# Opening of a bidirectional encoder layer: the first RMSNorm sums its squares over partitions in two groups of four chunks, and VectorE squares one of the chunks

## The chip, the cores and the metric

The kernel runs on one core of one Trainium2 chip. The metric is the device time of one execution in microseconds (us), shown as the median of several runs; the profile is of one further execution. Engines are called as in the profile: PE is TensorE's matmuls, PEld TensorE's weight loads, DVE is VectorE, ACT is ScalarE, POOL is GpSimd, SP is SyncE, which here does nothing but issue DMAs.

## The reference

One layer with 512 tokens of width 1024, all float32. Three sublayers each begin with an RMSNorm whose output is scaled and shifted by vectors computed from a conditioning vector c:

```python
c_act = silu(c)
mod = c_act @ w_mod + b_mod
sh1, sc1, g1, sh2, sc2, g2, sh3, sc3, g3 = split(mod, 9)
h = rmsnorm(x, norm_ffn1) * (1 + sc1) + sh1      # the opening
x = x + 0.5 * g1 * swiglu(h, w_ffn1_in, w_ffn1_out)
# then two gated attention mixers on one normalised input, then a second SwiGLU like the first
# rmsnorm(x, g) = x * rsqrt(mean(x * x, axis=-1) + 1e-6) * g
```

The change touches only the sum of squares of the very first RMSNorm.

## The kernel before, in words

The residual stream lies with features on partitions: eight chunks `x[0]` to `x[7]`, each of 128 features by 512 tokens. A sum over the 1024 features of a token is therefore a sum over eight chunks and then over 128 partitions. The sum over partitions is done by PE: `Norm.sums` (L321) takes a chunk of squares, 128 tokens at a time, as the weights and a two-column tile of ones as the moving operand, so a call is four matmuls of two columns each into the bank `tp`. Every float32 matmul shows as two passes in the trace, so a call is eight weight loads and eight matmuls there.

The opening (L586 to L648) is written out by hand: under a manual schedule PE, DVE, ACT, SP and POOL take their instructions in the order of the code. The steps:

- SP issues the loads of the eight chunks (L224), then those of the columns of `w_mod` (L234) and of the first weights (L191); ACT's queue issues the loads of c and of the parameters.
- PE spreads c over all partitions by two matmuls with one row (L590), and then does twelve matmuls of the identity by itself, whose result nobody reads (`warm(12)`, L596). They stand in PE's queue ahead of the sums.
- ACT squares the eight chunks, one after the other as they land (L631). DVE adds each square to the running sum (L633), so that one chunk of sums is left. In between DVE does four small operations on parameters (L250, L255).
- ACT applies silu to the spread c (L636); the result `cact` goes to a scratch in memory by a DMA from POOL (L637), and DVE needs it for every column.
- PE sums the one chunk over partitions (L638, through L326), does six more `warm` matmuls, and waits.
- ACT scales the sums (L305), POOL raises them to the power -0.5 (L306), PE spreads the result `rs` over partitions through the identity (L315).
- DVE meanwhile computes columns of the conditioning (`mod_col`, L269): SC1 of chunk 0 and SH1 of chunk 0; then a tiny copy of `rs` (L643), which makes it wait for POOL; then SC1 of chunk 1; and then the first operation of the hidden activations (L335).
- ACT rounds that result (L336), and PE starts on the first products of the first SwiGLU (L654). The eight chunks of the hidden activations follow in the same manner (`first_chunk`, L661).

Buffers: `sq` takes a tile of the ring `f2` of eight tiles for each chunk.

Of the kernel before, what the change touches and what calls it, by code (L numbers as in the profile page):

```python
# [14 lines left out]
AF = mybir.ActivationFunctionType  # L15
ALU = mybir.AluOpType
# [108 lines left out]
def layer(ctx: ExitStack, tc: tile.TileContext, a: dict):  # L125
    nc = tc.nc
    V, S, G, PE = nc.vector, nc.scalar, nc.gpsimd, nc.tensor
# [11 lines left out]
    def xt():  # L139
        return sbuf("x", [P, T], F32, 8)  # L140

    def f2():
        return sbuf("f2", [P, T], F32, F2)
# [61 lines left out]
    FULL = (slice(0, T),)  # L205
# [15 lines left out]
    x = [xt() for _ in range(NC)]  # L221
# [38 lines left out]
    def mod_col(v, c, w=None):  # L260
        if w is None:
            w = mod_load(v, c)
        t, b = modv[v][:, c : c + 1], mod_begin(v)[:, c : c + 1]
        cact = at_c[0]
        if v in norms:
            by = par[:, norms[v] + c : norms[v] + c + 1]
        else:
            by = 1.0 if v in (SH1, SH2, SH3) else -0.5 if v == G1 or v == G3 and c % 4 < 2 else 0.5
        summed = V.tensor_tensor_reduce(  # L269
            out=w, in0=w, in1=cact, scale=by, scalar=b, op0=ALU.mult, op1=ALU.add, accum_out=t,  # L270
        )
        if len(at_c) > 1:
            tc.keep_in_program_order(summed)
# [354 lines left out]
    n1 = Norm()  # L628
    for c in range(NC):
        sq = f2()  # L630
        S.activation(sq, x[c], AF.Square)  # L631
        if c:
            V.tensor_tensor(sq, sq, before, ALU.add)  # L633
        before = sq
    for i in range(2):
        S.activation(cact[:, i * T : (i + 1) * T], cb[i], AF.Silu)  # L636
    G.dma_start(c_scr, cact[0:1, :])  # L637
    n1.sums(sq, FULL[0], True, True)  # L638
    mod_col(SC1, 0, w1[0][0])
    rs = n1.rstd(FULL[0], S)  # L640
    first_split(0)
# [978 lines left out]
    x = [xt() for _ in range(NC)]  # L1620
# [375 lines left out]
```

## Time and profile before

| what | value |
|---|---|
| median of 3 runs | 1053.09 us |
| lowest, highest | 1052.79, 1056.16 us |
| the profiled execution, its time | 1054.45 us |
| its span (first to last instruction) | 1052.7 us |
| PE busy | 1037.4 us, 99% of the span |
| DVE, ACT, POOL busy | 75%, 56%, 14% |
| DMA moved | 214.07 MB, mean 203 GB/s |

The profile holds a page with the busy time of each engine, and views that can be asked of the trace: instructions in order of time (start, duration, engine, line, operation, output<-inputs, count, and in brackets the idle time before and what ended it), a table of who waited for whom, and the chain of work that ended last, followed back from the end. Times are counted from the start of the span; the profiled execution's own time is 1.75 us longer than the span. Ends of matmuls are modelled, so for PE the starts are the better measure. An engine that is idle off the chain costs nothing.

### The profile page before, as it was taken

Reading aid. Unit: us, or ns where it says so; the run is one execution under the profiler, and the core shown is the slowest. Engines: PE = TensorE matmul, PEld = TensorE weight load, DVE = VectorE, ACT = ScalarE, POOL = GpSimd, SP = SyncE. Lnnn points to the kernel's source line nnn. Section 1 sums busy time; section 2 is a strip of 40 time slices with the busy share of each in tenths; the row PEclk is TensorE's granted clock in tenths of the full one; section 3 lists DMA queues with packets and bytes.
Section 4 is the critical chain, followed back from the end, with each engine's and each line's share of the span. In section 5 each row is a group of like instructions: output and inputs, shape, how many; then the busy total and the mean of one; then the engine's idle time right before and its main releaser. Section 6 shows DMA issues by size and latency. Waiting matters only on the chain.

```text
span 1052.7 us, 18398 instructions
## 1 busy us (share of the span) xinstructions
PE 1037.4 (99%) x7216; PEld 952.2 (90%) x7216; DVE 792.9 (75%) x1421; ACT 591.3 (56%) x976; POOL 151.7 (14%) x166
## 2 busy tenths in 40 slices
PE   8999999999999999999999999999999999999997
PEld 6799899989998988888888888989999999999997
DVE  7988767687967844677964778995888777877777
ACT  6565235424653443787755878435867545655553
POOL 1100001001001100441012401001111111111210
PEclk9999999999999999999999999999999999999999
DMA  9977886788666384785358875795578999999964
GB/s 353 364 211 231 255 247 145 203 290 199 176 200 210 131 268 142 159 195 114 89 172 203 217 181 149 280 323 132 111 177 197 236 250 198 206 236 210 210 137 125
DMA packets 64760, 214.07 MB, mean 203 GB/s; under 512 B 7713, under 2 KB 9889, under 8 KB 64674
## 3 DMA queue, kind: packets, MB, share of 16 engines
q1 hardware_dynamic: 43920, 143.63, 39.7%
q0 software_dynamic: 18304, 65.02, 33.9%
q10 hardware_dynamic: 2450, 4.25, 1.1%
q8 instruction: 56, 0.92, 0.4%
q14 instruction: 30, 0.25, 0.1%
HBM read 203.96 MB, written 8.92 MB: 202 GB/s over the span
## 4 chain that ended last, share of the span: by engine, by line
PE 88%; DVE 5%; ACT 3%; DMA 1%; issue 1%; POOL 1%; SPq 0%; DVEq 0%; ACTq 0%; POOLq 0%
PE acc L436 7%; PE acc L434 7%; PE acc L435 7%; PE sc L436 6%; PE sc L434 6%; PE sc L435 6%; PE sc L166 5%; PE sc L164 5%; PE sc L165 5%; PE acc L164 3%; PE acc L165 3%; PE acc L166 3%; PE acc L1148 2%; PE acc L1150 2%; PE acc L1149 2%; PE tp L1199 1%
## 5 line engine op out<-in xcount | busy, mean ns | idle before, releaser
L436 PE MATMUL acc<-b,low 128*128 128x256 f32 x614 | 170.1, 277 | 0.2 <-DVE low L170 0.2
L434 PE MATMUL acc<-b,high 128*128 128x256 f32 x614 | 170.0, 277 | 0.1
L435 PE MATMUL acc<-b,high 128*128 128x256 f32 x614 | 169.9, 277 | 0.2 <-DVE b L1776 0.2
L434 PE MATMUL sc<-b,high 128*128 128x256 f32 x542 | 149.9, 277 | 1.2 <-DVE f L516 1.2
L436 PE MATMUL sc<-b,low 128*128 128x256 f32 x542 | 150.0, 277 | 0.1
L435 PE MATMUL sc<-b,high 128*128 128x256 f32 x542 | 149.8, 276 | 0.0
L436 PEld LDWEIGHTS acc<-b,low 128*128 128x128 f32 x614 | 115.3, 188 | 0.7 <-DVE low L170 0.6
L435 PEld LDWEIGHTS acc<-b,high 128*128 128x128 f32 x614 | 115.3, 188 | 0.5 <-DVE b L1776 0.4
L434 PEld LDWEIGHTS acc<-b,high 128*128 128x128 f32 x614 | 115.4, 188 | 0.4 <-issue 0.3
L434 PEld LDWEIGHTS sc<-b,high 128*128 128x128 f32 x542 | 101.8, 188 | 1.4 <-issue 1.3
L436 PEld LDWEIGHTS sc<-b,low 128*128 128x128 f32 x542 | 101.7, 188 | 0.3 <-DVE low L801 0.3
L435 PEld LDWEIGHTS sc<-b,high 128*128 128x128 f32 x542 | 101.8, 188 | 0.0
L164 PE MATMUL sc<-b,high 128*128 128x512 f32 (+1 forms) x272 | 99.1, 364 | 0.0
L166 PE MATMUL sc<-b,low 128*128 128x512 f32 (+1 forms) x272 | 98.8, 363 | 0.2 <-DVE low L895 0.2
L165 PE MATMUL sc<-b,high 128*128 128x512 f32 (+1 forms) x272 | 98.9, 364 | 0.0
L482 DVE TENSOR_TENSOR low<-raw,high 128x1024 fp32r<-128x1024 f32 (+1 forms) x60 | 70.2, 1187 | 34.9 <-ACT high L481 34.8
L164 PE MATMUL acc<-b,high 128*128 128x512 f32 (+1 forms) x200 | 72.6, 363 | 0.2 <-DVE f L1597 0.2
L482 DVE TENSOR_TENSOR low<-u,high 128x1024 fp32r<-128x1024 f32 (+1 forms) x47 | 55.8, 1188 | 22.4 <-ACT high L481 22.2
L166 PE MATMUL acc<-b,low 128*128 128x512 f32 (+1 forms) x200 | 71.8, 359 | 0.0
L165 PE MATMUL acc<-b,high 128*128 128x512 f32 (+1 forms) x200 | 71.8, 359 | 0.0
L269 DVE CUSTOM_DVE_ANT_0 u<-u,ka,begin 128x1024 f32<-128x1024 f32 x45 | 58.6, 1310 | 12.4 <-DMA u<-w_mod 12.3
L481 ACT CAST high<-raw 128x1024 fp32r<-128x1024 f32 (+1 forms) x60 | 59.6, 1021 | 0.3 <-PE acc L435 0.3
(403 smaller groups left out, 2791.4 us busy)
## 6 DMA issues: line engine op xcount, KB each, us to landing
u<-w_mod SPq DMA_DIRECT2D x66, 512.0 KB, 6.0
raw<-w2i SPq DMA_DIRECT2D x31, 512.0 KB, 5.2
u<-w2i POOLq DMA_DIRECT2D x31, 512.0 KB, 7.4
raw<-w1u SPq DMA_DIRECT2D x27, 512.0 KB, 5.7
u<-w1u POOLq DMA_DIRECT2D x18, 512.0 KB, 7.7
raw<-w1o SPq DMA_DIRECT2D x16, 512.0 KB, 4.4
raw<-w_gate SPq DMA_DIRECT2D x16, 512.0 KB, 4.1
low<-w_gate POOLq DMA_DIRECT2D x13, 512.0 KB, 7.3
```

The costliest lines, as they stand in the source:

```text
L164: PE.matmul(out, wh, xh, start=first, stop=False)
L165: PE.matmul(out, wh, xl, start=False, stop=False)
L166: PE.matmul(out, wl, xh, start=False, stop=last)
L269: summed = V.tensor_tensor_reduce(out=w, in0=w, in1=cact, scale=by, scalar=b, op0=ALU.mult, op1=ALU.add, accum_out=t,)
L434: PE.matmul(out, wh[:, s], xh, start=first and j == 0, stop=False, skip_group_check=True)
L435: PE.matmul(out, wh[:, s], xl, start=False, stop=False, skip_group_check=True)
L436: PE.matmul(out, wl[:, s], xh, start=False, stop=last and j == 1, skip_group_check=True)
L481: S.copy(hi, t)
L482: V.tensor_tensor(lo, t, f(hi), ALU.subtract)
L1148: PE.matmul(out[t][:, 0:n], hh[k][:, ht], wh[:, o : o + n], start=k == 0, stop=False)
L1149: PE.matmul(out[t][:, 0:n], hh[k][:, ht], wl[:, o : o + n], start=False, stop=False)
L1150: PE.matmul(out[t][:, 0:n], hl[k][:, ht], wh[:, o : o + n], start=False, stop=k == NC - 1)
```

## The change

The fourth chunk (c is 3) is squared by DVE instead of ACT. The running sum of squares starts anew at the fifth chunk (c is 4), so that there are two partial sums: of chunks 0 to 3 and of chunks 4 to 7. Each is summed over partitions by itself: `n1.sums` is called once inside the loop, right after the fourth chunk, which opens the accumulation, and once at its old place, which closes it.

```diff
     for c in range(NC):
         sq = f2()
-        S.activation(sq, x[c], AF.Square)
-        if c:
+        if c == 3:
+            V.tensor_tensor(sq, x[c], x[c], ALU.mult)
+        else:
+            S.activation(sq, x[c], AF.Square)
+        if c % 4:
             V.tensor_tensor(sq, sq, before, ALU.add)
         before = sq
+        if c == 3:
+            n1.sums(sq, FULL[0], True, False)
     for i in range(2):
         S.activation(cact[:, i * T : (i + 1) * T], cb[i], AF.Silu)
     G.dma_start(c_scr, cact[0:1, :])
-    n1.sums(sq, FULL[0], True, True)
+    n1.sums(sq, FULL[0], False, True)
     mod_col(SC1, 0, w1[0][0])
```

Five lines are added, so lines behind the loop are numbered five higher in the changed kernel.

PE's order from the start of the program to the spread of `rs` (`sc` and `tp`, `op` are banks, `f_…` the chunk of squares, `sm` the tile of `rs`), before:

```order
L590 MATMUL sc_121<-u_2_76,ones 128x512
L590 MATMUL sc_122<-u_2_76,ones 128x512
L596 MATMUL sc_125<-ident 128x128 x12
L326 MATMUL tp_183<-ones,f_37_177 128x2 x4
L596 MATMUL sc_197<-ident 128x128 x6
L315 MATMUL op_204<-ident,sm_189 128x128 x4
```

And with the change:

```order
L590 MATMUL sc_121<-u_2_76,ones 128x512
L590 MATMUL sc_122<-u_2_76,ones 128x512
L596 MATMUL sc_125<-ident 128x128 x12
L326 MATMUL tp_168<-ones,f_33_165 128x2 x4
L326 MATMUL tp_168<-ones,f_38_181 128x2 x4
L596 MATMUL sc_200<-ident 128x128 x6
L315 MATMUL op_207<-ident,sm_192 128x128 x4
```

Four matmuls of two columns are added behind the twelve `warm` matmuls, and those of the old place stand behind them.

DVE's order from its first addition to the first column, before:

```order
L633 TENSOR_TENSOR f_31_159<-f_31_159,f_30_157 128x512
L250 SCALAR_TENSOR_TENSOR begin<-par 128x8
L255 TENSOR_SCALAR begin<-par 128x2x2
L633 TENSOR_TENSOR f_32_162<-f_32_162,f_31_159 128x512
L255 TENSOR_SCALAR begin<-par 128x2x2
L633 TENSOR_TENSOR f_33_165<-f_33_165,f_32_162 128x512
L633 TENSOR_TENSOR f_34_168<-f_34_168,f_33_165 128x512
L633 TENSOR_TENSOR f_35_171<-f_35_171,f_34_168 128x512
L633 TENSOR_TENSOR f_36_174<-f_36_174,f_35_171 128x512
L633 TENSOR_TENSOR f_37_177<-f_37_177,f_36_174 128x512
L269 ISA u_21_138,mod_97<-u_21_138,ka_112,begin,par 128x1024
```

And with the change:

```order
L636 TENSOR_TENSOR f_31_159<-f_31_159,f_30_157 128x512
L250 SCALAR_TENSOR_TENSOR begin<-par 128x8
L255 TENSOR_SCALAR begin<-par 128x2x2
L636 TENSOR_TENSOR f_32_162<-f_32_162,f_31_159 128x512
L632 TENSOR_TENSOR f_33_165<-x_81 128x512
L255 TENSOR_SCALAR begin<-par 128x2x2
L636 TENSOR_TENSOR f_33_165<-f_33_165,f_32_162 128x512
L636 TENSOR_TENSOR f_36_175<-f_36_175,f_35_173 128x512
L636 TENSOR_TENSOR f_37_178<-f_37_178,f_36_175 128x512
L636 TENSOR_TENSOR f_38_181<-f_38_181,f_37_178 128x512
L269 ISA u_21_138,mod_97<-u_21_138,ka_112,begin,par 128x1024
```

DVE still does seven operations on 128x512 tiles: the square of the fourth chunk (L632, reading `x_81`) has come, and the addition that joined the fifth chunk to the running sum has gone. On ACT one of the eight squares has gone; nothing else is moved.

## The prediction

> **What bounds the kernel now.** The page comes first: PE is busy nearly throughout.
>
> ```profile
> span 1052.7 us, 18398 instructions
> PE 1037.4 (99%) x7216; PEld 952.2 (90%) x7216; DVE 792.9 (75%) x1421; ACT 591.3 (56%) x976; POOL 151.7 (14%) x166
> ```
>
> Of the 15.3 us that PE is idle (1052.7 - 1037.4), the table of waits (waiter, releaser, total us, times, longest) puts these among the five longest:
>
> ```profile
> PE sc L590 <- DMA u<-c: 2.3, 1, 2.3
> PE acc L654 <- ACT b L336: 1.4, 2, 0.8
> ...
> PE op L315 <- POOL sm L306: 0.9, 1, 0.9
> ```
>
> All three lie in the opening. So the opening is a chain in front of a PE-bound kernel, and what it gains or loses passes to the end if nothing behind absorbs it. The chain of waits for the first 30 us (start, duration, what):
>
> ```profile
> 2.32 3.75 PE sc L590 x4
> 6.07 5.26 PE sc L596 x24
> 11.33 0.85 PE tp L326 x8
> 12.18 0.02 issue
> 12.20 0.27 ACT sm L305
> 12.48 0.08 issue
> 12.56 1.87 POOL sm L306
> ...
> 14.53 1.17 DVE u L269
> 15.70 0.09 issue
> 15.79 0.09 DVE mod L269
> 15.88 0.66 DVE b L335
> ...
> 29.42 0.67 DVE b L335
> ```
>
> The reader is to see what stands ahead of the sums (L326): not DVE's additions (L633), but the twelve `warm` matmuls (L596). Behind the sums come ACT, POOL, and then DVE up to 30 us, without a DMA. The last gap of the opening on PE, from the instructions in order of time:
>
> ```profile
> 30.89 0.50 PE L654 MATMUL acc<-b,high 128*128 128x512 f32 x1 [0.56 <-ACT b L336]
> ```
>
> From there the chain runs on PE's own products.
>
> Whether DVE or PE holds the sums back is the question on which this change hangs, since both are ready within a tenth of a microsecond. PE, its weight loads, and DVE in order of time:
>
> ```profile
> 6.00 5.33 PE L596 MATMUL sc<-ident 128*128 128x128 f32 x24
> 10.64 0.69 PE L596 MATMUL sc<-ident 128*128 128x128 f32 x3
> 11.17 1.00 PE L326 MATMUL tp<-ones,f 128*128 128x2 f32 x8
> 12.03 1.58 PE L596 MATMUL sc<-ident 128*128 128x128 f32 x12
> 11.11 0.97 PEld L326 LDWEIGHTS tp<-ones,f 128*128 128x128 f32 x8
> 12.00 0.53 PEld L596 LDWEIGHTS sc<-ident 128*128 128x128 f32 x4
> 7.18 3.88 DVE L633 TENSOR_TENSOR f<-f,f 128x512 f32<-128x512 f32 x5 [0.70 <-ACT f L631]
> 10.37 0.69 DVE L633 TENSOR_TENSOR f<-f,f 128x512 f32<-128x512 f32 x1
> 10.97 1.34 DVE L269 CUSTOM_DVE_ANT_0 u<-u,ka,begin 128x1024 f32<-128x1024 f32 x1
> ```
>
> DVE's last addition ends at 10.37 + 0.69 = 11.06. The `warm` passes run back to back from 6.00; the last three lie from 10.64 to 11.33 by the modelled ends, and the weight loads of the sums begin at 11.11 with no idle time in front. So before the change both releases came together, and the sums cannot start before about 11.1 even if DVE were done long before.
>
> **The change part by part.** *ACT loses one square.* Its row, the transfers that it waits for, and ACT's two silus behind:
>
> ```profile
> 6.52 3.32 ACT L631 ACTIVATE f<-x 128x512 f32<-128x512 f32 x5 [0.85 <-DMA x<-x]
> 9.21 0.63 ACT L631 ACTIVATE f<-x 128x512 f32<-128x512 f32 x1
> 9.75 1.07 ACT L636 ACTIVATE ka<-sc 128x512 f32<-128x512 f32 x2
> L224 SPq DMA_DIRECT2D x<-x x8: 382/430/432, 0.7 to 4.0; - x8
> DMA to landing us min/median/max: 2.8/4.4/5.2
> ```
>
> The last chunk is issued at 4.0 and the longest transfer takes 5.2 us, so it lands near 9.2, where ACT's last square starts (9.21). The five squares from 6.52 start (9.21 - 6.52) / 4 = 0.67 us apart, although one takes 0.63: they follow the landings. So taking one away leaves ACT's last square at 9.21 to 9.84 and its silus at 9.75 to 10.82. I take 0 for this part; its other bound would be 0.63 earlier, if the chunks lay there already.
>
> *DVE takes one square and drops one addition.* The square of chunk 3 needs only its landing, 6.52. An addition in a row costs (3.88 - 0.69) / 4 = 0.80 us from start to start. The square starts at 6.52, the addition of chunk 3 near 7.4 (0.80 and the small L255 between), that of chunk 5 when ACT has squared it (6.52 + 3 x 0.67 = 8.53), those of chunks 6 and 7 0.80 apart, 9.33 and 10.13. The last ends at 10.82, a quarter of a microsecond before 11.06. The first column (L269 at 10.97) needs ACT's silu, which ends at 10.82 as before, so it doesn't move.
>
> *PE gets four more matmuls of two columns.* They need the sum of chunks 0 to 3, ready near 8.1, but stand behind the `warm` matmuls and so start at 11.11. Eight passes take from 11.11 to 12.00 in the weight-load rows: 0.89 us. The old call then starts at 12.00 instead of 11.11; its data is there since 10.82. It ends 0.89 us later. Nothing hides this term: PE is the chain here. DVE's quarter microsecond is worth nothing, because PE isn't free to use it.
>
> *What is queued behind.* The rows of the engines that wait:
>
> ```profile
> 12.20 0.27 ACT L305 ACTIVATE sm<-tp,eps 128x4 f32<-128x4 f32 x1 [1.39 <-PE tp L326]
> 14.33 1.04 ACT L614 CAST high<-raw 128x1024 fp32r<-128x1024 f32 x1 [1.86 <-DMA raw<-w1s]
> 12.56 1.86 POOL L306 TENSOR_TENSOR sm<-sm,half 128x4 f32<-128x4 f32 x1 [0.78 <-ACT sm L305]
> 14.45 0.17 DVE L643 COPY sm<-sm 128x4 f32<-128x4 f32 x1 [0.93 <-POOL sm L306]
> 14.47 1.16 PE L315 MATMUL op<-ident,sm 128*128 128x128 f32 x8 [0.86 <-POOL sm L306]
> 17.35 0.50 PE L654 MATMUL acc<-b,high 128*128 128x512 f32 x1 [0.83 <-ACT b L336]
> ```
>
> ACT was idle for 1.39 before L305, and its next work, L614, waits for a DMA until 14.33: L305 at 13.09 to 13.36 still fits in front. POOL's power goes from 12.56 to 13.45, DVE's copy, for which DVE sat idle 0.93, from 14.45 to 15.34, the column and L335 behind it too, and PE's first product from 17.35 to 18.24. L614 ends at 15.37, long before ACT's next turn, so it absorbs nothing. From 14.5 to 30.9 the chain runs on DVE work and two waits on it; no step of it waits for a clock or a transfer that stays in place. So 0.89 arrives at 30.89 and passes to the end.
>
> *The sum.* 0 + 0 + 0.89, about +0.9 us. The profiled execution would have a span of 1053.6 and a time of 1054.45 + 0.9 = 1055.3; its time was 1.36 above the median, so for the median I forecast 1053.09 + 0.9 = 1054.0.
>
> *Bounds of the added matmuls.* The unknown is how fast PE runs when it reaches them. The 24 early passes go at about (10.64 - 6.00) / 22 = 0.21 us each, the twelve later ones at 1.58 / 12 = 0.13. If the early passes ran at 0.13 in another execution, they would end at 9.1, the first sums at 10.0, and the second would start with DVE, 10.82 against 11.1: -0.3 us. If the eight new passes ran at 0.21, they would cost 1.7. I take 0.89, measured at just this place, and keep -0.3 and +1.7 as ends. The granted clock doesn't explain the two rates:
>
> ```profile
> 6.00:11.00 5.00, 5.00 (x24) 5.00 (x24) 3.88 (x8) 4.12 (x7) 0.00 (x0) 1.00 0.98 379
> ```
>
> PEclk, third from the end, reads 1.00 over the slow stretch. [...] The pace of these rows agrees with a doubling near 11.0, which the granted clock alone would not tell. [...]
>
> **The rivals.** *PE speeds up earlier* than in this profile. For it: the rate changed just before the sums, so it can't be a fixed property of the place. Against: only one execution is seen. Between the ends -0.3 and +0.9 its middle is +0.3: 1053.4. [...]
>
> *DVE was what held the sums,* and the quarter microsecond is won, without a price on PE: 1053.09 - 0.25 = 1052.8. For it: the last addition ends 0.05 us before the sums' first weight load. Against: the passes of L596 lie without a gap up to the same moment.
>
> *Something behind absorbs it:* 1053.1. For it: the opening's DMA share is near 1 (0.98 in the row above) and a transfer that keeps its time would take the delay as slack. Against: no DMA in the chain from 2.32 to 30.89.
>
> *PE stays slow longer (slower than before).* Matmuls of two columns do little work; if the doubling came only after the sums and the spread, the sixteen passes would take 16 x 0.21 = 3.4 in place of 0.89, +2.5, the spread (L315) 8 x 0.21 = 1.7 in place of 1.16, +0.5, and if the slow stretch then lasted some 5 us into the first products, as long as that from 6.00 to 11.1, half of it is lost but for the gap of 0.56 before 30.89: +1.9. Together +4.9: 1058.0. It decides only if the doubling falls behind 17. Against: PE is as busy up to 11.1 as before, and the rate had risen by then.
>
> **How the numbers follow.** Forecast (+0.9) 0.60, earlier speed-up 0.17, absorbed 0.10, DVE's gain 0.06, slow PE 0.05, something else 0.02. Predicted 1054.0. The costs give 1052.8 to 1054.8; the three runs shown lie up to 3.1 above the median and 0.3 below, so a new median can lie a microsecond or so off: 1052.3 to 1056.2. A measurement of this kernel can tell about 0.3%, 3.2 us, from no change. All cases but the slow PE lie within that; with a little for scatter: faster 0.02, same 0.92, slower 0.06.
>
> **What would show it.** In the changed profile the two calls of L326 should stand back to back from 11.1, sixteen passes in 1.8 us, with no wait on DVE; the last addition should end at 10.6 to 10.9; L305, L306 and the first product should each be 0.9 later (13.1, 13.45, 18.2), and PE's gap near 31 should be as before. If the second call starts after an idle PE, DVE held it and the forecast's reason is wrong. If the first product is at 17.4 or earlier, PE's pace differed. If the first product is 0.9 later and the end isn't, it was absorbed.

## The result and the profile after

The changed kernel took 1057.64 us in the median of 22 runs (1052.89 to 1059.34), against 1054.44 us (1052.03 to 1058.33) for the kernel before in the same set. The ratio of the means is 1.0024, 95% interval [1.0014, 1.0033]: slower, by some 2.5 us in the mean and 3.2 us in the median. The forecast was 0.9 us slower, 1054.0, and its range ended at 1056.2. It started from the median of three runs, 1053.09, which lies 1.35 below the 22 runs' median of the same kernel; that is part of the miss, but not all: moved up by 1.35, the range would end at 1057.55.

The profiled execution of the changed kernel took 1056.2 us:

```profile
span 1054.4 us, 18410 instructions
PE 1036.9 (98%) x7224; PEld 952.0 (90%) x7224; DVE 792.6 (75%) x1421; ACT 590.7 (56%) x975; POOL 150.8 (14%) x166
```

PE is as busy as before (1037.4 us) and the span is 1.7 us longer: the time has gone into waits. The larger ones are not where the change is. The opening, in order of time:

```profile
6.58 4.31 PE L596 MATMUL sc<-ident 128*128 128x128 f32 x24
10.72 1.84 PE L326 MATMUL tp<-ones,f 128*128 128x2 f32 x16
14.29 1.16 PE L315 MATMUL op<-ident,sm 128*128 128x128 f32 x8 [0.28 <-POOL sm L306]
17.16 0.50 PE L659 MATMUL acc<-b,high 128*128 128x512 f32 x1 [0.83 <-ACT b L336]
8.45 2.28 DVE L636 TENSOR_TENSOR f<-f,f 128x512 f32<-128x512 f32 x3 [0.25 <-ACT f L634]
12.06 1.28 DVE L269 CUSTOM_DVE_ANT_0 u<-u,ka,par 128x1024 f32<-128x1024 f32 x1
14.27 0.17 DVE L648 COPY sm<-sm 128x4 f32<-128x4 f32 x1 [0.92 <-POOL sm L306]
12.61 0.27 ACT L305 ACTIVATE sm<-tp,eps 128x4 f32<-128x4 f32 x1 [1.85 <-PE tp L326]
12.96 1.27 POOL L306 TENSOR_TENSOR sm<-sm,half 128x4 f32<-128x4 f32 x1 [1.24 <-ACT sm L305]
```

The two calls stand back to back, sixteen passes in 1.8 us, as forecast, and L305 starts 0.41 later than before (12.61 against 12.20). But POOL's operation ends at 14.23, where it ended at 14.42 before, and the first product starts at 17.16 instead of 17.35. POOL's operation was 1.86 us long and is 1.27 now.

Four waits have grown. The first stands ahead of everything: PE waits for the load of c 2.9 us, where it waited 2.3.

```profile
PE sc L590 <- DMA u<-c: 2.9, 1, 2.9
```

This has nothing to do with the change: over the profiles of all kernels here it lies between 2.2 and 3.0, and two profiles of the same kernel differ as much. The second is at the end of the opening: DVE waits for a column of `w_mod`, and PE's gap near 31 grows from 0.56 to 1.22. The changed kernel's other three profiles don't have it (0.53 to 0.55).

```profile
27.47 1.28 DVE L269 CUSTOM_DVE_ANT_0 u<-u,ka,par 128x1024 f32<-128x1024 f32 x1 [0.59 <-DMA u<-w_mod]
```

The third lies in the second SwiGLU. The table of waits of PE, of the change:

```profile
PE sc L434 <- DVE f L516: 2.3, 1, 2.3
```

and of before:

```profile
PE sc L434 <- DVE f L516: 1.2, 1, 1.2
```

The chain of waits shows what leads there, with the change:

```profile
763.97 1.24 DVE low L482
...
765.49 8.97 DMA u<-w2i
...
774.55 1.06 ACT high L481
775.64 1.23 DVE low L482
...
777.47 0.61 DVE f L516
```

and before:

```profile
764.43 1.24 DVE low L482
...
765.96 7.89 DMA u<-w2i
...
773.94 1.06 ACT high L481
775.03 1.23 DVE low L482
...
776.86 0.61 DVE f L516
```

POOL issues a DMA that adds one block of `w2i` to another in place (`G.dma_start` with `accum_op`, in `Unit.prepare`). It took 8.97 us instead of 7.89. ACT and DVE then round the sum into its high and low parts (L481, L482). DVE's addition L516, which lets PE go on, is queued behind L482, though it doesn't need it. So each microsecond of that transfer beyond 6.72 is a microsecond of PE's: in the profiles in which it ends the wait, it took 7.01, 7.31, 7.89, 8.09, 8.14 and 8.97 us, and PE waited 0.29, 0.59, 1.17, 1.37, 1.42 and 2.25 us.

The fourth lies near 1037 us, behind a transfer of the same kind (`w2o`). The table of waits from 1030 us on has, with the change,

```profile
ACT high L481 <- DMA u<-w2o: 5.7, 2, 3.5
PE sc L436 <- DVE low L482: 0.5, 1, 0.5
PE sc L434 <- ACT high L481: 0.2, 1, 0.2
```

and before, where no wait of PE stands in that stretch,

```profile
ACT high L481 <- DMA u<-w2o: 4.5, 2, 3.6
```

The last such transfer took 6.02 us with the change and 4.84 before. Of the longer span, 1.08 us arise at the wait near 778 and 1.06 near 1037, counted by the starts of the same matmuls; elsewhere PE lost and won smaller amounts that come to 0.4 us less.

### The profile page after: what moved, and what is told of

Its sections match the earlier page's. It is cut to its first block, busy times and chain, and to the rows that moved or that the text cites. A ratio compares the mean times of both kernels' runs of the same rounds, so it can differ in the third digit from the quotient of the medians.

```text
span 1054.4 us, 18410 instructions
## 1 busy us (share of the span) xinstructions
PE 1036.9 (98%) x7224; PEld 952.0 (90%) x7224; DVE 792.6 (75%) x1421; ACT 590.7 (56%) x975; POOL 150.8 (14%) x166
## 4 chain that ended last, share of the span: by engine, by line
PE 74%; issue 10%; DVE 5%; DMA 5%; ACT 3%; POOL 2%; POOLq 0%; DVEq 0%; ACTq 0%; SPq 0%
PE sc L166 5%; PE sc L164 5%; PE sc L165 5%; PE acc L436 4%; PE acc L434 4%; PE acc L435 4%; PE sc L436 4%; PE sc L434 4%; PE sc L435 4%; PE acc L164 3%; PE acc L165 3%; PE acc L166 3%; PE acc L1155 2%; PE acc L1153 2%; PE acc L1154 2%
## 5 line engine op out<-in xcount | busy, mean ns | idle before, releaser
L436 PE MATMUL acc<-b,low 128*128 128x256 f32 x614 | 170.1, 277 | 0.2 <-DVE low L170 0.2
L436 PE MATMUL sc<-b,low 128*128 128x256 f32 x542 | 150.0, 277 | 0.6 <-DVE low L482 0.5
L436 PEld LDWEIGHTS acc<-b,low 128*128 128x128 f32 x614 | 115.3, 188 | 0.6 <-DVE low L170 0.5
L436 PEld LDWEIGHTS sc<-b,low 128*128 128x128 f32 x542 | 101.8, 188 | 1.0 <-DVE low L482 0.7
L482 DVE TENSOR_TENSOR low<-raw,high 128x1024 fp32r<-128x1024 f32 (+1 forms) x60 | 70.2, 1186 | 34.6 <-ACT high L481 34.5
L482 DVE TENSOR_TENSOR low<-u,high 128x1024 fp32r<-128x1024 f32 (+1 forms) x47 | 55.7, 1187 | 24.9 <-ACT high L481 24.6
L481 ACT CAST high<-u 128x1024 fp32r<-128x1024 f32 (+1 forms) x47 | 48.0, 1023 | 22.7 <-DMA u<-w2i 8.0
```

Source lines behind the costliest of these rows:

```text
L436: PE.matmul(out, wl[:, s], xh, start=False, stop=last and j == 1, skip_group_check=True)
L481: S.copy(hi, t)
L482: V.tensor_tensor(lo, t, f(hi), ALU.subtract)
```

## Experiments

Sixteen experiments were run with eleven kernels, all but the last timed in 11 or 12 runs and set against the kernel before on the same chip. Single runs of one kernel scatter by several microseconds, and the question turned out to be how often a run is long; so the number of runs above 1056.5 us is told too. Over all sets the kernel before has 18 of 154 such runs (and 1 of 12 as the control below), and the changed kernel 29 of 58. Two executions of 2 and 6 ms, in two of the sets, are left out of these counts.

**Controls.** The kernel before, and the changed kernel three more times.

> The kernel before, unchanged, as a control: how its times scatter and which granted clock each of its runs has. The changed kernel's 22 runs go from 1052.9 to 1059.3, and those with a mean granted clock of 0.998 or less are the longer ones (1057.1 and above). Theory A (the added matmuls of two columns let PE's clock fall again in some executions): here most runs have 0.999 or 1.000 and lie near 1052 to 1055, and few lie at 0.998. Theory B (the change moves a transfer or a wait and the clock is a bystander): the mix of clocks is the same as with the change, and at the same clock this kernel is 2 to 3 us faster.

> The changed kernel, unchanged, on the same chip as the control. Ratio near 1.0024, +2.5 us. Theory A: the runs fall in two groups by clock, about two thirds at 0.998 or less and 3 to 4 us longer than the rest, and the rest are within 1 us of the control's. Theory B: one group, all some 2.5 us longer than the control at the same clock.

> The changed kernel once more, so that it stands beside the next one on the same chip. Theory C (the added TensorE instructions move the fetches of code, and these delay parts of transfers): a ratio near 1.001 to 1.0025, with several runs above 1056.5 us.

> The changed kernel beside these: about half of its runs above 1056.5 us, ratio 1.001 to 1.0025.

| kernel | median us | ratio to before, 95% interval | runs above 1056.5 |
|---|---|---|---|
| before, as control | 1053.91 | 1.0000 [0.9986, 1.0015] | 1 of 12 |
| changed, second set | 1055.36 | 1.0009 [0.9992, 1.0025] | 4 of 12 |
| changed, third set | 1056.42 | 1.0020 [1.0003, 1.0036] | 6 of 12 |
| changed, fourth set | 1055.49 | 1.0014 [1.0001, 1.0027] | 5 of 12 |

The loss has the same sign each time, 1 to 2.5 us by the ratios, though the second set's interval includes no change. The profile of the second set fell on a long run (1058.24 us), and shows most of what makes it long. PE's list, and the windows (length, then busy times of PE, PEld, DVE, ACT, POOL, then the granted clock, DMA share and GB/s):

```profile
778.22 0.43 PE L434 MATMUL sc<-b,high 128*128 128x256 f32 x1 [2.25 <-DVE f L516]
775.00:778.20 3.20, 0.97 (x9) 0.78 (x8) 2.55 (x4) 1.14 (x2) 0.00 (x0) 1.00 1.05 202
778.40:781.80 3.40, 3.40 (x17) 3.40 (x17) 2.26 (x5) 2.75 (x4) 0.00 (x0) 0.51 0.11 20
```

The same transfer took 8.97 us again, PE waited 2.25 us again, and then the granted clock fell to half for 3.4 us. The first profile of the change, with the same wait, kept its clock, and has 31 matmuls in the second window instead of 17:

```profile
778.40:781.80 3.40, 3.40 (x31) 3.40 (x31) 2.26 (x4) 2.77 (x5) 0.00 (x0) 1.00 0.16 30
```

Half the clock for 3.4 us is a loss of some 1.7 us, an estimate from these windows (0.49 x 3.4). So the wait costs twice in some executions: by itself, 2.25 us here, and by the clock. The mean granted clocks fit: of the changed kernel's 29 long runs 24 have 0.998 or less, of its 29 others one. That is the two groups of theory A; its reason, that the clock falls at the narrow sums, isn't borne out, because the fall seen is the one behind the wait near 778.

**The parts of the change apart.**

```diff
# split without the square: ScalarE squares all eight chunks
-        if c == 3:
-            V.tensor_tensor(sq, x[c], x[c], ALU.mult)
-        else:
-            S.activation(sq, x[c], AF.Square)
+        S.activation(sq, x[c], AF.Square)
# square without the split: VectorE squares chunk 3; one running sum, one call
-        if c % 4:
+        if c:
...
-        if c == 3:
-            n1.sums(sq, FULL[0], True, False)
...
-    n1.sums(sq, FULL[0], False, True)
+    n1.sums(sq, FULL[0], True, True)
```

> The two groups of sums without VectorE's square: ScalarE squares all eight chunks, the running sum starts anew at the fifth, and the sums over partitions are taken twice. Theory A: the same mix of clocks as the changed kernel and +2 to +3 us. The theory that VectorE's square or ScalarE's missing one costs the time: as before, within 0.5 us.

> VectorE squares the fourth chunk, but there is one running sum over all eight chunks and one call that sums over partitions, as before. VectorE has one operation of 0.69 us more. Theory A: clocks as in the control and the time within 0.8 us of it. The theory that VectorE's square costs the time: +2 to +3 us here.

> The two groups of sums without VectorE's square, once more. It has the changed kernel's TensorE instructions, yet only 1 of its 12 runs was above 1056.5 us, where the changed kernel had 24 of 46 and the kernel before 11 of 97. Theory C in its plain form (the shift of TensorE's code alone makes the long runs): 4 to 8 of 12 long, ratio 1.001 to 1.0025. Theory H (it takes the shift of the code together with the earlier start that VectorE's square gives the opening): 0 to 2 of 12 long, ratio 1.000 to 1.001.

The split alone: 1.0003 [0.9988, 1.0018] and, again, 1.0006 [0.9991, 1.0020], with 1 and 3 of 12 runs above 1056.5. The square alone: 1.0005 [0.9990, 1.0019], 1 of 12. The 3 of the split's second set lie between theory H's forecast (0 to 2) and theory C's (4 to 8). Neither part is clearly slower by itself, and neither interval excludes 1.5 us, about what the changed kernel lost in these sets (1.0009 and 1.0014). So the times of these kernels neither bear out nor exclude that one part carries the whole loss.

**TensorE's instructions without the sums.** The change adds 16 instructions (eight weight loads, eight matmuls) to TensorE's stream. These kernels add as many, or take as many away, in dummy matmuls behind the sums, where PE waits for POOL and for the first product.

```diff
# more: the kernel before        # fewer: the changed kernel
-    warm(6)                     -    warm(6)
+    warm(8)                     +    warm(4)
     rb_op = n1.spread(rs)            rb_op = n1.spread(rs)
-    warm(4)                     -    warm(4)
+    warm(6)                     +    warm(2)
```

> The kernel before with two dummy matmuls added to each of the two groups behind the sums (six become eight, four become six): the same number of TensorE instructions as the change adds, none of them in front of the sums, in gaps of TensorE. Theory C: +1 to +2.5 us, the transfer near 765 us takes about 8.9 us and the wait near 778 us is about 2.2 us. Theory D: as before within 0.5 us.

> The kernel before with four dummy matmuls more behind the sums, once more (5 of 11 runs were above 1056.5 us, ratio 1.0023). Theory C: again 4 to 8 of 12 long and a ratio of 1.001 to 1.0025. Theory H: the first result was chance, 0 to 2 of 12 long and a ratio below 1.001.

> The changed kernel with two of the dummy matmuls taken from each of the two groups behind the sums (six become four, four become two). They lie in gaps of TensorE, so the opening should keep its times; TensorE's stream of instructions then has the same length as before the change, and the blocks in which its code is fetched (16 KB, one every 15 us or so) fall at the same places of the program as before. Theory C (the shifted fetches lengthen the accumulating transfer issued near 765 us, which keeps TensorE waiting near 778 us): that transfer takes 7.0 to 7.9 us as before, the wait is 0.3 to 1.2 us instead of 2.25, and the time is that of before within 0.7 us. Theory D (the opening's shift in time against the transfers does it): as the changed kernel, 8.9 us and +1 to +2.5 us.

> The changed kernel with four dummy matmuls fewer behind the sums, once more, beside the changed kernel. Theory C: 1 to 2.5 us faster than the changed kernel, ratio 0.999 to 1.0005, few runs above 1056.5 us. Theory D (the shift of the opening in time): the same as the changed kernel within 0.5 us.

More, twice: 1.0023 [1.0009, 1.0036] and 1.0020 [1.0004, 1.0035], 5 of 11 runs above 1056.5 each time. Four dummy matmuls, with the sums and the squares untouched, cost what the change costs. Their first profile has PE's first product no later than before, but a longer wait of DVE for `w_mod` further on, and behind it this gap of PE, which the second profile lacks (0.55):

```profile
28.26 1.28 DVE L269 CUSTOM_DVE_ANT_0 u<-u,ka,par 128x1024 f32<-128x1024 f32 x1 [2.07 <-DMA u<-w_mod]
32.16 0.50 PE L654 MATMUL acc<-b,high 128*128 128x512 f32 x1 [2.77 <-ACT b L336]
```

Fewer, twice: 1.0004 [0.9990, 1.0018] and 1.0007 [0.9993, 1.0021], 2 of 12 runs above 1056.5 each time; beside the changed kernel of the same set it is 1.4 us faster in the median, with an interval of the means' difference from -0.7 to 2.9. That points the same way and doesn't settle it, because with fewer dummy matmuls the clock was low more often: a mean granted clock of 0.998 or less in 8 of the 12 runs, beside 4 of the changed kernel's 12 (below, on the clock). None of these four profiles is of a long run, and theory C's forecast for the transfer near 765 (8.9 us with more, 7.0 to 7.9 with fewer) is not seen in them: 6.6 and 6.0 us with more, 6.3 and 8.1 with fewer.

**The wait near 778 us taken away.** The sum that POOL's transfer makes there (`s4` of the third unit) is rounded one product later, so that L516 comes ahead of it in DVE's queue; PE needs it only later.

```diff
-                    due.append((starts[n] - PRODUCT * ahead[q] - 0.01, len(due), do, q))
+                    by = 1 if ahead is MAKE and q == "s4" and u is units[2] else ahead[q]
+                    due.append((starts[n] - PRODUCT * by - 0.01, len(due), do, q))
```

> The changed kernel; in the second SwiGLU one weight sum is rounded one product later (the s4 of the third unit), so that the rounding that waits for the accumulating transfer near 765 us no longer stands in VectorE's and ScalarE's queues ahead of the addition that frees TensorE's bank near 778 us. Theory E (what the change costs is that wait, and the fall of the clock that it brings in some executions): no wait over 0.3 us near 778, mean granted clock 0.999 to 1.000 in nearly all runs, 1052 to 1053.5 us, no longer than the kernel before with the same edit. Theory F (the cost lies in the opening): still +1 to +2.5 us over that one.

> The kernel before with the same later rounding. Theory E: 0.5 to 1.2 us faster than before (its wait near 778 was 0.6 and 1.2 us in two profiles), about 1052.5, and fewer long runs. Theory F: the same gain, and the changed kernel with this edit stays 1 to 2.5 us behind it.

> The changed kernel with four dummy matmuls fewer and with the later rounding in the second SwiGLU: the code is fetched where it was before the change, and the wait near 778 us is gone. Theories C and E together: as fast as the kernel before with the later rounding or a little faster, 1052.5 to 1053.3 us, no run above 1056. If the sums themselves cost time in the opening, 0.5 to 1 us more than that.

> The same with the later rounding in the second SwiGLU. Theory E (the long runs come from the wait near 778 us): no run above 1056, the median 0.5 to 2.5 us below the one without the later rounding, close to 1053.3. If long runs come from elsewhere, as many as without it.

| kernel, with the later rounding | median us | ratio to before, 95% interval | runs above 1056.5 |
|---|---|---|---|
| before | 1053.30 | 0.9995 [0.9986, 1.0003] | 0 of 12 |
| changed | 1053.96 | 1.0002 [0.9992, 1.0013] | 0 of 12 |
| changed, fewer dummy matmuls | 1053.08 | 0.9989 [0.9978, 1.0000] | 0 of 11 |
| before, more dummy matmuls | 1054.07 | 1.0000 [0.9990, 1.0010] | 0 of 12 |

Of 47 runs none is above 1056.5, whichever opening they have, as theory E forecast; the changed kernel's median lies half a microsecond above its 1052 to 1053.5. DVE's list of the changed kernel with this edit shows why: L516 no longer waits behind the rounding.

```profile
773.60 0.68 DVE L516 TENSOR_TENSOR f<-f,sc 128x512 f32<-128x512 f32 x1
...
778.46 1.22 DVE L482 TENSOR_TENSOR low<-u,high 128x1024 fp32r<-128x1024 f32 x1
```

In PE's table of waits L516 has gone from the top, and these rows lead:

```profile
PE sc L591 <- DMA u<-c: 2.8, 1, 2.8
PE acc L660 <- ACT b L336: 1.3, 2, 0.8
PE op L164 <- DVE x L1406: 0.8, 1, 0.8
```

Between the changed kernel and the kernel before, both with the edit and on one chip, 0.66 us of the median remain (0.94 of the mean, interval 0.5 to 1.4). The wait near 1037 is not touched by this edit: the changed kernel's profile still has it (L436 for L482, 0.5 us), and PE is 0.65 us later behind it; the profile of the kernel before has none.

**POOL and VectorE.** DVE's second column is moved behind the copy that waits for POOL.

```diff
-    mod_col(SH1, 0, w1[0][1])
     V.tensor_copy(small(NT), rs)
+    mod_col(SH1, 0, w1[0][1])
```

> The kernel before, with VectorE's second column (SH1 of chunk 0) moved behind the tiny copy that waits for POOL, so that VectorE is idle while POOL raises to the power -0.5. Theory G (POOL's operation cannot run while VectorE works on a column, and so ends 0.9 us after the column whenever the sums come): POOL's operation takes 0.9 to 1.1 us instead of 1.86 and ends at 13.4 to 13.6 instead of 14.42. If its length is its own: 1.86 as before, ending at 14.4.

One profile, without a comparison of times:

```profile
12.63 1.04 POOL L306 TENSOR_TENSOR sm<-sm,half 128x4 f32<-128x4 f32 x1 [0.27 <-ACT sm L305]
13.70 0.17 DVE L642 COPY sm<-sm 128x4 f32<-128x4 f32 x1 [0.94 <-POOL sm L306]
```

With DVE idle the operation takes 1.04 us, not 1.86, and ends at 13.67, 0.75 sooner. It takes the same 1.04 in the changed kernel's profiles of the third and fourth set, where it starts at 13.84 and 14.15, behind the end of DVE's second column (13.30 and 12.94). So some 0.8 us of its length in the kernel before go with DVE's column beside it. What makes the one wait for the other no run here shows.

## Why the prediction was wrong

- *The added calls stand behind the `warm` matmuls and lengthen the chain on PE.* Right: 16 passes without a gap from 10.72. DVE's last addition (8.45 + 2.28 = 10.73) is needed only by the second eight of them.
- *ACT's missing square gains nothing, DVE's chain a quarter of a microsecond.* Right: 10.73 against 11.06; the columns start at 10.79 instead of 10.97.
- *POOL's power goes from 12.56 to 13.45 and everything behind it by as much: this step failed.* It took 1.86 us for the operation's own length. As the run with the column moved shows (1.04 us instead of 1.86), POOL was waiting for DVE's second column, and it ended 0.9 us after that column in both profiles: 12.24 + 1.28 = 13.52 to 14.42 before, 12.06 + 1.28 = 13.34 to 14.23 with the change. So the sums had 0.8 us of cover (14.42 less the 1.04 us that POOL takes with DVE idle, less 12.56), of which the change used 0.4 in its first profile, and the quarter microsecond won on DVE, taken as worthless, moved the columns and came through to PE: the first product was 0.19 sooner in that execution.
- *How fast PE runs when it reaches the sums was named as the unknown, with an earlier speed-up as a rival.* Right: the passes sped up, from one weight load in 0.21 us to one in 0.11, about 9.5 us into the span in the first profile of the change, near 11.0 in that of before, and only near 12 in those of the third and fourth set; over all profiles here the record of the granted clock begins between 9.3 and 12.6 (at 9.47 and 11.04 in the first two). Why the moment differs no run shows. In the third and fourth set the cover is exceeded:

```profile
13.84 1.04 POOL L306 TENSOR_TENSOR sm<-sm,half 128x4 f32<-128x4 f32 x1 [2.14 <-ACT sm L305]
17.80 0.50 PE L659 MATMUL acc<-b,high 128*128 128x512 f32 x1 [0.82 <-ACT b L336]
```

  That is the third set: 0.45 later than the 17.35 of before, 0.76 in the fourth (18.11). The control's is 17.40, and the two profiles of the split alone have 18.40 and 17.06. So the opening came out between 0.2 us shorter and 0.8 longer with the change, by when the passes speed up and by when c has landed, which lets PE begin (2.26 in the third set, 3.01 in the fourth).
- *From 30.89 on PE sets the pace and a shift passes to the end unchanged: this step failed, and it is the one that put the result outside the range.* The chain behind the opening is PE's for most of its length, but it hangs on accumulating transfers whose time isn't fixed (near 765 us from under 6 to 9.0 us in the profiles here, near 1031 from 4.6 to 6.0), and on a clock that fell to 0.51 for 3.4 us in one profile after such a transfer had kept PE waiting for 2.25 us. What came through to the end was therefore not the 0.89 of the opening: 1.08 us arose near 778 and 1.06 near 1037 in the first profile of the change. The prediction quoted no row behind 31 us; the table of PE's waits had L516 with 1.2 us in third place, and the prediction's "..." passed over it. No rival said that a change of the opening could lengthen a wait 750 us later. The sentence that no step up to 30.89 waits for a transfer held by little, too: in the first profile of the change DVE waited 0.59 us for `w_mod` there.
- *The rival of a slow PE* had the right kind of loss, half a clock (0.51 from 778.40 to 781.80 in the profile of the second set), at the wrong place: not in the opening, but behind the wait at 778.
- *That a measurement can tell about 0.3%* was too wide: 22 runs of each kernel gave an interval of 0.1% to either side, and so a change of 0.24% shows.

So of the loss of 1 to 2.5 us, the larger share goes over the wait near 778: with that wait taken away the medians differ by 0.66 us instead of 1.8 to 3.2, and no long runs are left. The rest has the size that the prediction gave to the added matmuls, and that is luck: the profiles put it near 1037, and dummy matmuls behind the sums leave much the same (with the later rounding a ratio of 1.0000 to the kernel before without it, in another set, beside the changed kernel's 1.0002).

**What the number of TensorE instructions does, and what stays open.** The trace shows code being loaded by DMA, on a queue of its own:

```profile
q8 instruction: 56, 0.92, 0.4%
```

That is 16 KB at a time. By an estimate from these sizes, 0.92 MB over 2 x 7216 instructions of TensorE is 64 bytes each, so a load would hold 256 of them; that the queue is TensorE's rests on this estimate. Near 1031 its place follows the number of TensorE instructions. In the ten profiles of kernels with sixteen more (changed, split alone, more dummy matmuls, and two of these with the later rounding) a load begins 1.5 to 2.1 us after the last transfer of `w2o` is issued, that transfer takes 5.1 to 6.0 us, and PE waits at L436 for 0.2 to 0.5 us. In the eight profiles of kernels with the old number (before, square alone, column moved, fewer dummy matmuls, and two of these with the later rounding) the load begins 3.9 to 4.4 us after it, the transfer takes 4.6 to 5.0 us, and none has that wait. Both groups hold old and changed openings, so it is the number of instructions and not the shift of the start in time that brings this wait. That the load itself slows the transfer fits, but the trace doesn't tell a packet's engine.

Why these few instructions make the transfer near 765 long more often stays open. The load of code ahead of it begins at 757.1 and 757.0 in two profiles of before, and at 754.9, 755.7, 755.1 and 757.0 in the four of the change. The transfer reports 16 parts. In the two profiles of before, 15 had landed by 771.9 and the last came at 773.9, or 14 by 771.6 and the last two at 772.6 and 773.1; in the first profile of the change 14 had by 771.5 and the last two came at 774.3 and 774.5; in one of the split all had by 772.0. So a few parts are late, not the whole. But the length doesn't follow the place of the load: the changed kernel's four profiles give 9.0, 9.0, 6.0 and 7.7 us, and the split alone, which has the changed kernel's TensorE instructions, had only 4 long runs of 24, beside 9 of 24 of the changed kernel in the same sets. No run here tells at that place a shift of the code from a shift of the start in time.

## What to carry to other kernels

Before a delay in one stage is carried to the end, look through the chain behind it for waits on transfers whose length varies (here from under 6 to 9.0 us near 765), and count them as places where a small shift can grow, even one of the number of instructions alone: above all where an operation that frees the busiest engine is queued behind one that waits for a DMA (L516 behind L482, up to 2.25 us of PE's here). Where a small operation is oddly long (L306 with 1.86 us), compare it with its other instances and with what the engine beside it does at the time (1.04 with DVE idle); its excess may be cover, as the 0.8 us here, up to which a delay ahead of it was free. For effects of a quarter of a percent, single profiles mislead: the first profile of the change had a sooner start of the products, and the number of long runs told more than a median, and a wait that comes with every profile of one group and none of the other told more than either.

## What the runs showed that was not expected

- Behind a wait of 2.25 us of TensorE the granted clock fell to half for 3.4 us in one profile (0.51 from 778.40 to 781.80), and not in another with the same wait (1.00 over the same window). With one profile of each, why only one of the two fell is not shown.
- The granted clock was seen at half in the opening too, with four dummy matmuls fewer (and the later rounding). One profile has it at 1.00 from 13.0 to 15.9 us and at 0.50 from 16.0 to 22.7, in windows as above:

```profile
13.00:15.90 2.90, 2.42 (x21) 2.23 (x21) 0.92 (x4) 1.31 (x2) 1.04 (x1) 1.00 1.03 414
16.00:22.70 6.70, 5.96 (x20) 4.89 (x19) 6.36 (x9) 4.66 (x7) 0.92 (x1) 0.50 1.03 410
23.00:30.00 7.00, 7.00 (x32) 5.77 (x31) 7.00 (x11) 3.49 (x5) 0.00 (x0) 1.00 1.04 335
```

  The first products ran 6.7 us at half clock, in a run of 1056.04 us where that kernel's median is 1053.08. Of its 11 runs 5 have a mean granted clock of 0.998 or less; with all dummy matmuls, and that rounding, it is 1 of 12. But the square alone, with all of them, has it in 5 of 12, so that dummy matmuls guard against such a fall is not shown.
- The later rounding, a change of one line far from the opening, makes the times steadier with either opening: 1052.65 to 1054.60 in 12 runs with the opening of before, against 1051.97 to 1058.06 for the kernel before in the same set. In the median it gains no more than its measurement can tell (0.9995 [0.9986, 1.0003]).
